# A hybrid S5 / stick-breaking attention block: the scan's preparation in smaller steps, a shorter attention period, and reordered operands in the first up block

## The chip, the cores and the metric

One core of one Trainium2 chip. The metric is the device time of one execution in microseconds (us).

## The reference

One decoder block over 528 positions (512 tokens behind 16 meta tokens), 2048 channels, all in float32:

```python
hn = rmsnorm(h, norm_mix_g[i])
proj = hn @ w_in[i]                       # u 1024 | q k v 1024 each
y_ssm = s5_mixer(u, ...)                  # 64 groups: complex scan of 64 states, GELU, GLU gate
y_attn = stick_breaking_attention(q, k, v).reshape(bsz, L, ATTN_WIDTH)   # 16 heads of 64
mixed = jnp.concatenate([rmsnorm(y_ssm, g_ssm_out[i]), rmsnorm(y_attn, g_attn_out[i])], axis=-1)
h = h + mixed @ w_out[i]
hn = rmsnorm(h, norm_ffn_g[i])
up = causal_depthwise_conv(hn @ w_up[i], conv_w[i], conv_b[i])   # 2 x 5632
gate, val = jnp.split(up, 2, axis=-1)
h = h + (jax.nn.silu(gate) * val) @ w_down[i]
out = rmsnorm(h, norm_final_g)
```

The scan is `h_t = a h_(t-1) + Bbar u_t` with a complex `a` for each state, and `y = Re(C h) + d u`. The attention's weight of a key is `exp(log_sigmoid(z) + sum of log_sigmoid(-z) over the later valid keys)`.

## The kernel before

**Matmuls.** Activations lie with channels on the partitions and positions along the free axis. A float32 product is made of three fp32r matmuls (`mm3`, L317 to L320), which the text calls a triple: high part of the weight by high part of the activation (L318), high by low (L319), low by high (L320). A weight block of 128x1024 is fetched by SyncE's queue (L196), its high part `wh` is a cast on ScalarE (`split_hi`, L240), its low part `wl` a subtraction on VectorE (`split_lo`, by the helper `sub`, L115). `split_high` (L396, ScalarE) and `split_low` (L400, VectorE) do the same for activations that are multiplied by a gain. The helpers at L103 (an activation), L106 (add or subtract), L109 (multiply), L112 (add) and L115 (subtract) record most other operations, so many rows have their lines.

**Order.** Nothing is scheduled by a planner: the order in which the code emits instructions is the order of each engine's queue. The dense work (w_in, w_glu, w_out, up, w_down) is a stream of triples, and beside it runs a lane of other work, written as Python generators. Each triple of which the index in its block is under 7 adds 1.4 times its width to a credit, and when the credit reaches the period, one step of the lane is emitted:

```python
def pulse(ns):
    if hold[0]:
        return
    credit[0] += ns
    while credit[0] >= period[0]:
        credit[0] -= period[0]
        if lanes:
            step()
```

The first lane is the scan (`ssm_lane`, period `PERIOD` = 1600), which begins inside the first blocks of w_in; the second is the attention (`att_lane`, period `PERATT` = 1100); the third makes the operands of the up products (`x_lane`, `PERX` = 1100). Steps rest while the last two blocks of q and the w_glu blocks run. `drain()` (L1298), behind the first half of w_out (the half that multiplies the scan's output), emits all steps that are left of the lanes at once; the second half of w_out multiplies the attention's output.

**Scan.** 64 groups in eight mains `j` of eight groups. `ssm_prep(j)` (L666 to L724) makes the tables of a main on VectorE: rotations `E[c]` (L109 and L106) with a mirrored copy on ScalarE (L103), the decay tile `Dk` (L687), then by `cplx` (L691 ff) four complex products HB[0], HB[1], PB[0], PB[1], each two multiplications (L109) and a sum (L106) into a tile `x` and two ScalarE copies (L704) that set the sum into place; `BB` is set by ScalarE too (L103). `ssm_main(j)` (L726 to L828) transposes PB[0] and PB[1] on TensorE (L735, two times four, each into a bank of PSUM of the pool `z`), copies them out (L737), multiplies, scans on VectorE, multiplies again into Y (L821 to L823), takes the GELU (L103) and stores. A main emits five steps of the next main's preparation: four `next(ahead, None)` between its own steps and the rest by `for _ in ahead: pass` at its end.

**Attention.** Four units of 12 items. `stage_a` makes an item's scores (mask matmul L937, then L953); two steps later `stage_a2` subtracts, scans and subtracts on VectorE (L115 with `at<-z`, L975, L978), which frees the scores' bank; two more steps later `stage_b` transposes (L995, L1005) into a bank of the same pool; then come `stage_c` (L1020, L1044) and `stage_d`. Behind the last item stands the normalisation over 1024 channels: `acc_square` squares on ScalarE and adds on GpSimd (L112), `rms_steps` (L357 to L379) sums over the partitions (L363), takes logarithm and exponent on ScalarE and finishes on VectorE (L367, L374, L109, L379); then for each of eight tiles, one step each, `yatt` is multiplied by the result (L109) and split (L396, L400).

**Up.** The up product runs in 44 blocks f of seven products each (`PROD`: 11, s1, s2, s4, s3, 12, 22), in which sums of weight blocks and of activation blocks are multiplied. In block 0 the sums of activations are made as the block runs: `x_hi` (L1335) casts a high part on ScalarE, `x_lo` (L115) makes a low part on VectorE, sums (L1325, L1330, L115) come ahead of both. In between stands the FFN's normalisation, stepped by `next(norm, None)`.

## Time and profile before

| | |
|---|---|
| median of 3 runs | 2241.73 us (2240.02 to 2243.7) |
| the profiled execution | 2240.49 us |
| its span in the profile | 2238.7 us, 39814 instructions |
| mean granted clock of TensorE | 0.989 of full speed |
| TensorE busy (matmuls / weight loads) | 97% / 92% of the span |
| VectorE busy | 70% |
| ScalarE busy | 47% |
| GpSimd busy | 10% |
| DMA | 335.11 MB, mean 150 GB/s |

The page gives each engine's busy time over the whole span. The list of waits says for what an engine stood still, by the line that waited and the line that released it. A table by stretches gives busy time and granted clock of a part of the span; a clock of 1.00 is full speed. The timeline gives single instructions with start and length, where rows of one line that follow each other are drawn together (x2, x4). A timeline's bracket is the idle time of the engine in front of a row and what ended it.

### The profile page before, as it was taken

What the parts mean: (1) busy time and instruction counts of PE and PEld (TensorE: products, weight loads), DVE (VectorE), ACT (ScalarE), POOL (GpSimd) and SP (SyncE); (2) the same over time, 40 slices, a digit from 0 to 9 for tenths busy, and PEclk for the clock granted to TensorE, in tenths of its full rate; (3) what the DMA queues carried; (4) which work ended last, traced back from release to release, by engine and by line L of the source; (5) the groups of instructions that cost most, each with busy time, mean ns of one, the idle gap of its engine ahead of it and who ended that gap; (6) DMA issues with size and microseconds to landing.
All of it is one profiled execution on the core that took longest, in us unless ns stands there. A gap on an engine that the chain in (4) does not pass through costs nothing.

```text
span 2238.7 us, 39814 instructions
## 1 busy us (share of the span) xinstructions
PE 2170.9 (97%) x16196; PEld 2057.8 (92%) x16196; DVE 1574.1 (70%) x2395; ACT 1042.1 (47%) x1664; POOL 227.6 (10%) x354
## 2 busy tenths in 40 slices
PE   8979999999998999999999999999999999999997
PEld 8979999999897998999999999999999888888887
DVE  7957776775887768887788778877888544444464
ACT  6243443665664445555555555555545222222235
POOL 0000000001222230111011101111110000000004
PEclk9989999999999999999999999999999999999999
DMA  6423223324333256777777677777776533333342
GB/s 214 121 78 100 96 91 111 143 96 143 110 95 109 100 161 169 196 202 188 193 198 203 185 195 199 202 184 196 195 204 189 193 127 116 112 121 116 119 141 76
DMA packets 118807, 335.11 MB, mean 150 GB/s; under 512 B 13024, under 2 KB 25696, under 8 KB 118624
## 3 DMA queue, kind: packets, MB, share of 16 engines
q1 hardware_dynamic: 100288, 269.56, 37.0%
q0 software_dynamic: 17472, 61.89, 13.5%
q8 instruction: 127, 2.08, 0.4%
q10 hardware_dynamic: 864, 1.11, 0.2%
q14 instruction: 56, 0.46, 0.1%
HBM read 300.23 MB, written 32.28 MB: 149 GB/s over the span
## 4 chain that ended last, share of the span: by engine, by line
PE 80%; DVE 4%; ACT 2%; issue 2%; DMA 0%; POOL 0%; DVEq 0%; ACTq 0%; POOLq 0%
PE d L319 19%; PE d L318 19%; PE d L320 19%; PE z L319 4%; PE z L318 4%; PE z L320 4%; PE y L319 2%; PE y L318 2%; PE y L320 2%; PE z L953 1%; DVE wl L115 1%; PE z L1005 1%; PE y L1044 1%; DVE s L115 1%; DVE s L109 1%
## 5 line engine op out<-in xcount | busy, mean ns | idle before, releaser
L318 PE MATMUL d<-s,wh 128*128 128x258 f32 (+4 forms) x3376 | 1038.7, 308 | 14.1 <-ACT s L396 7.2
L319 PE MATMUL d<-s,wh 128*128 128x258 f32 (+4 forms) x3376 | 1033.3, 306 | 8.0 <-DVE s L115 6.4
L320 PE MATMUL d<-s,wl 128*128 128x258 f32 (+4 forms) x3376 | 1028.8, 305 | 0.0
L318 PEld LDWEIGHTS d<-s,wh 128*128 128x128 f32 x3376 | 639.0, 189 | 43.9 <-ACT s L396 7.5
L319 PEld LDWEIGHTS d<-s,wh 128*128 128x128 f32 x3376 | 642.1, 190 | 39.5 <-DVE s L115 7.9
L320 PEld LDWEIGHTS d<-s,wl 128*128 128x128 f32 x3376 | 642.8, 190 | 28.3 <-DVE wl L115 0.2
L240 ACT CAST wh<-wr 128x1024 fp32r<-128x1024 f32 (+2 forms) x209 | 197.5, 945 | 396.7 <-PE d L319 327.6
L115 DVE TENSOR_TENSOR wl<-wr,wh 128x1024 fp32r<-128x1024 f32 (+2 forms) x209 | 233.3, 1116 | 120.7 <-ACT wh L240 109.6
L112 DVE TENSOR_TENSOR s<-s,d 128x512 f32<-128x512 f32 (+2 forms) x176 | 103.4, 589 | 265.0 <-PE d L320 262.4
L319 PE MATMUL z<-s,wh 128*128 128x258 f32 (+1 forms) x752 | 214.9, 286 | 0.0
L318 PE MATMUL z<-s,wh 128*128 128x258 f32 (+1 forms) x752 | 214.1, 285 | 0.0
L320 PE MATMUL z<-s,wl 128*128 128x258 f32 (+1 forms) x752 | 213.2, 284 | 0.0
L318 PE MATMUL y<-s,wh 128*128 128x258 f32 (+1 forms) x640 | 182.9, 286 | 0.0
L319 PE MATMUL y<-s,wh 128*128 128x258 f32 (+1 forms) x640 | 182.3, 285 | 0.0
L320 PE MATMUL y<-s,wl 128*128 128x258 f32 (+1 forms) x640 | 181.1, 283 | 0.0
L115 DVE TENSOR_TENSOR wl<-wu,wh 128x1024 fp32r<-128x1024 f32 x132 | 161.4, 1223 | 5.8 <-ACT wh L240 5.6
L240 ACT CAST wh<-wu 128x1024 fp32r<-128x1024 f32 x132 | 138.9, 1053 | 32.7 <-ACT s L103 32.7
L112 POOL TENSOR_TENSOR s<-s,s 128x514 f32<-128x514 f32 (+1 forms) x73 | 83.3, 1144 | 683.0 <-ACT s L103 545.8
L319 PEld LDWEIGHTS z<-s,wh 128*128 128x128 f32 x752 | 144.5, 192 | 0.0
L320 PEld LDWEIGHTS z<-s,wl 128*128 128x128 f32 x752 | 144.2, 192 | 0.0
L318 PEld LDWEIGHTS z<-s,wh 128*128 128x128 f32 x752 | 142.4, 189 | 0.0
L115 DVE TENSOR_TENSOR wl<-wu_s,wh 128x1024 fp32r<-128x1024 f32 x88 | 107.9, 1226 | 41.4 <-ACT wh L240 41.4
(224 smaller groups left out, 2893.4 us busy)
## 6 DMA issues: line engine op xcount, KB each, us to landing
wu<-w_up SPq DMA_DIRECT2D x132, 512.0 KB, 5.1
wu_s<-w_up SPq DMA_DIRECT2D x88, 512.0 KB, 4.7
wu_s<-w_up POOLq DMA_DIRECT2D x88, 512.0 KB, 7.2
wr<-w_down SPq DMA_DIRECT2D x96, 384.0 KB, 3.0
wr<-w_in SPq DMA_DIRECT2D x63, 512.0 KB, 4.3
wr<-w_out SPq DMA_DIRECT2D x32, 512.0 KB, 3.7
fact<-s POOLq DMA_DIRECT2D x44, 256.0 KB, 2.7
s<-fact SPq DMA_DIRECT2D x44, 256.0 KB, 3.3
```

Source lines behind the costliest of these rows:

```text
L109: e.tensor_tensor(out, a, b, op=ALU.mult)
L112: e.tensor_tensor(out, a, b, op=ALU.add)
L115: e.tensor_tensor(out, a, b, op=ALU.subtract)
L240: S.copy(hi[:, r], raw[:, r])
L318: PE.matmul(ps, whi, xhi, start=start, stop=False, **kw)
L319: PE.matmul(ps, whi, xlo, start=False, stop=False, **kw)
L320: PE.matmul(ps, wlo, xhi, start=False, stop=stop, **kw)
L953: PE.matmul(zs[0][:, x, :], qq[:, i, r], kk[:, :k], start=False, stop=x == nh - 1 and i_ == 2, skip_group_check=True,)
L1005: PE.transpose(b[:, x, :], c[:, P * x : P * x + P], ident[:n, :n])
L1044: PE.matmul(yp[64 * i : 64 * i + 64, p, :], self.vts[p][0][:, t, 64 * i : 64 * i + 64], ws[2 * p + i][:, t, :], start=t == 0 and p == 0, s ...
```

## The change

Four edits. (1) `ssm_prep` is cut into `rotation`, `mirror`, `cplx`, `place` and `place_b`, and has seven steps where it had five: VectorE's sums are emitted one step ahead of the ScalarE copies that read them, with eight `x` tiles in place of four. Three idle steps (`SLACK`) follow the first preparation. In a main, the rest of the next main's preparation is emitted ahead of Y's matmuls, not behind the store. (2) `PERATT` is 950. (3) In the first up block the high parts are cast at j = 0 (before 2), the low parts are made at j = 2 (before 4), and the normalisation's steps begin with the second product. (4) `rms_steps` puts its two half rows into one 528-wide slot, three slots in place of six.

```diff
 NC4 = L // 4
 NEG = -1.0e30
 PERIOD = 1600.0
-PERATT = 1100.0
+PERATT = 950.0
+
+SLACK = 3
 PERX = 1100.0
 HOLD = True
 
...
         def rms_steps(out, acc, parts, width, pool=(psy, "y"), last=()):
 
             n = range(len(parts))
-            v, y, t = [[slot([P, 264])[:, : b - a] for a, b in parts] for _ in range(3)]
+            lo = parts[0][0]
+            v, y, t = [[x[:, a - lo : b - lo] for a, b in parts] for x in [slot([P, 528]) for _ in range(3)]]
             for i, (a, b) in enumerate(parts):
                 ps = bank([P, b - a], *pool)
                 PE.matmul(ps, ones, acc[:, a:b], start=True, stop=not last)
...
             open_phase("ssm")
             yield from ssm_params(SP)
             yield from ssm_prep(0, SP)
+            for _ in range(SLACK):
+                yield
             for j in range(8):
                 while uready[0] <= j:
                     yield
...
             def v4(t):
                 return t.rearrange("p q (a b) -> p q a b", b=12)
 
-            for c in range(2):
+            def rotation(c):
                 ta, tb = slot([P, 4, 72]), slot([P, 4, 72])
                 mul(V, v4(ta), outer(P1[0], 3), outer(P0[c], 2))
                 mul(V, v4(tb), outer(P1[1], 3), outer(P0[1 - c], 2))
                 tt(V, E[c][:, :, MIR:], ta, tb, ALU.subtract if c == 0 else ALU.add)
+
+            def mirror(c):
                 act(E[c][:, :, MIR - 1 :: -1], E[c][:, :, MIR + 1 : 2 * MIR + 1], AF.Copy, scale=1.0 - 2.0 * c)
-                if c == 0:
-                    yield
-            Dk = slot([P, 4, NC4])
-            S.copy(Dk[:, :, 1:], sp["mag4"][:, qs].unsqueeze(2).to_broadcast([P, 4, NC4 - 1]))
-            G.memset(Dk[:, :, 0:1], 0.0)
-            yield
+
             full = [P, 4, 4, 16]
 
             def blk(t):
...
                     t[64 * x : 64 * x + 64].rearrange("p q (s i h) -> p s q i h", s=4, i=2)[:, :, :, x, :] for x in range(2)
                 ]
 
-            def cplx(c, a, b, out):
-
-                t = [small([P, 256], "x", bufs=4).rearrange("p (s q h) -> p s q h", q=4, h=16) for i in range(2)]
+            def cplx(c, a, b):
+
+                t = [small([P, 256], "x", bufs=8).rearrange("p (s q h) -> p s q h", q=4, h=16) for i in range(2)]
                 mul(V, t[0], a[0], b[c])
                 mul(V, t[1], a[1], b[1 - c])
                 tt(V, t[0], t[0], t[1], ALU.subtract if c == 0 else ALU.add)
+                return t[0]
+
+            def place(t, out):
+
                 for hf, r in enumerate(halves):
-                    S.copy(blk(out)[hf], t[0][r])
+                    S.copy(blk(out)[hf], t[r])
+
+            def place_b(c):
+                for x, r in enumerate(halves):
+                    b = sp["bbar"][c][r, qs, :]
+                    act(blk(BB[c])[x], b.unsqueeze(1).to_broadcast([64, 4, 4, 16]), AF.Copy, scale=1.0 - 2.0 * c)
 
             PB, HB, BB = sp["PB"], sp["HB"][j % 2], sp["BB"]
             rep = lambda t: t[:, qs, :].unsqueeze(1).to_broadcast(full)
             kk = [sp["AK"][:, c, 0:4, qs].unsqueeze(3).to_broadcast(full) for c in range(2)]
             rr = [sp["AR"][:, c, :, qs].unsqueeze(3).to_broadcast(full) for c in range(2)]
-            cplx(0, kk, [rep(t) for t in sp["c"]], HB[0])
-            yield
-            cplx(1, kk, [rep(t) for t in sp["c"]], HB[1])
-            for c in range(2):
-                cplx(c, rr, [rep(t) for t in sp["bbar"]], PB[c])
-                for x, r in enumerate(halves):
-                    b = sp["bbar"][c][r, qs, :]
-                    act(blk(BB[c])[x], b.unsqueeze(1).to_broadcast([64, 4, 4, 16]), AF.Copy, scale=1.0 - 2.0 * c)
-                if c == 0:
-                    yield
+            cc, bb = [rep(t) for t in sp["c"]], [rep(t) for t in sp["bbar"]]
+
+            rotation(0)
+            yield
+            rotation(1)
+            mirror(0)
+            Dk = slot([P, 4, NC4])
+            S.copy(Dk[:, :, 1:], sp["mag4"][:, qs].unsqueeze(2).to_broadcast([P, 4, NC4 - 1]))
+            G.memset(Dk[:, :, 0:1], 0.0)
+            yield
+            t0 = cplx(0, kk, cc)
+            mirror(1)
+            yield
+            place(t0, HB[0])
+            t0, t1 = cplx(0, rr, bb), cplx(1, kk, cc)
+            yield
+            place(t0, PB[0])
+            t0 = cplx(1, rr, bb)
+            place(t1, HB[1])
+            place_b(0)
+            yield
+            place(t0, PB[1])
+            place_b(1)
             bt.update(E=E, Dk=Dk, HB=HB)
             yield
 
...
             del loaded[j]
             if uready[0] > j + 1:
                 chunks_in(j + 1)
+            for _ in ahead:
+                pass
             Y = slot([P, 4, NC4])
             for x in range(2):
                 ps = bank([P, 2, NC4], psz, "z")
...
                     PE.matmul(ps[:, q, :], HB[1][:, qq, :], St[1][:, qq, :], start=False, stop=q == 1, skip_group_check=True)
                 act(Y[:, 2 * x : 2 * x + 2, :], ps, AF.Gelu_apprx_tanh)
             nc.sync.dma_start(ydram[j].rearrange("t x q c -> (t x) q c"), Y)
-            for _ in ahead:
-                pass
             yield
 
 
...
                     xh, xl = X[n][j]
                     mm3(ps, w[0][:, j, :], w[1][:, j, :], xh, xl, j == 0 and n in ("11", "s1", "12"), j == 7, skip_group_check=True)
 
+                    if f == 0 and i < 6 and j == 0:
+                        xs = [x_hi(p, PROD[i + 1]) for p in range(EARLY, 8)]
                     if f == 0 and i < 6 and j == 2:
-                        xs = [x_hi(p, PROD[i + 1]) for p in range(EARLY, 8)]
-                    if f == 0 and i < 6 and j == 4:
                         for y in xs:
                             x_lo(*y)
                         if i == 5:
                             xg.clear()
-                        next(norm, None)
+                        if i:
+                            next(norm, None)
                     if j == 3:
                         split_hi(pos[0] + 1)
                         prep(pos[0] + 2)
```

Lines of the changed kernel have other numbers: L704 is L710 there, L240 is L242, L103 is L105, L109 is L111, L112 is L114, L115 is L117, L400 is L403, L374 and L379 are L377 and L382. On TensorE the same rows are emitted; the first transposes L735 stand 20 triples later among the dense ones, the first unit of the attention 21 triples later, and the matmuls of the attention's normalisation 41 triples earlier: 45 triples ahead of the end of the first half of w_out, where there were 4. The attention lane now ends inside that half, and `drain()` finds nothing to emit.

ScalarE, the preparation inside one of the first mains (`s_1505` to `s_1508` are PB and HB tiles, `s_1511` and `s_1512` BB, `wh` a weight's high part, the last two rows the GELU of Y). Before:

```order
L704 COPY s_1507<-x_2913 64x4x4x16 x2
L240 CAST wh_2961<-wr_2743 128x1024
L240 CAST wh_3029<-wr_2857 128x1024
L704 COPY s_1508<-x_3091 64x4x4x16 x2
L704 COPY s_1505<-x_3098 64x4x4x16 x2
L103 ACTIVATE s_1511<-s_1229 64x4x4x16 x2
L240 CAST wh_3113<-wr_2965 128x1024
L704 COPY s_1506<-x_3128 64x4x4x16 x2
L103 ACTIVATE s_1512<-s_1230 64x4x4x16 x2
L103 ACTIVATE s_3151<-z_3152 128x264
L103 ACTIVATE s_3151<-z_3160 128x264
```

The same place in the change (PB and HB are `s_1502` to `s_1505`, BB `s_1508` and `s_1509`):

```order
L242 CAST wh_3010<-wr_2776 128x1024
L242 CAST wh_3078<-wr_2883 128x1024
L242 CAST wh_3146<-wr_3014 128x1024
L710 COPY s_1504<-x_2980 64x4x4x16 x2
L710 COPY s_1502<-x_3161 64x4x4x16 x2
L710 COPY s_1505<-x_3166 64x4x4x16 x2
L105 ACTIVATE s_1508<-s_1226 64x4x4x16 x2
L710 COPY s_1503<-x_3185 64x4x4x16 x2
L105 ACTIVATE s_1509<-s_1227 64x4x4x16 x2
L105 ACTIVATE s_3223<-z_3224 128x264
L105 ACTIVATE s_3223<-z_3232 128x264
L242 CAST wh_3253<-wr_3082 128x1024
```

The three casts stand together ahead of the copies, the copies follow each other without a cast between, and the sums that they read have been emitted a step earlier on VectorE.

VectorE, the end of the attention: last operations of the normalisation (`rstd`), then the eight tiles (`s<-s,rstd` is the multiplication, `vec` the split L400). Before, in one lump behind the first half of w_out:

```order
L379 SCALAR_TENSOR_TENSOR rstd_8893<-s_8898,s_8896 128x258
L379 SCALAR_TENSOR_TENSOR rstd_8893<-s_8899,s_8897 128x256
L109 TENSOR_TENSOR s_8079<-s_8079,rstd_8893 128x514
L109 TENSOR_TENSOR s_8080<-s_8080,rstd_8893 128x514
L400 SCALAR_TENSOR_TENSOR s_8934<-s_8079,vec,s_8933 128x514
L109 TENSOR_TENSOR s_8701<-s_8701,rstd_8893 128x514
L400 SCALAR_TENSOR_TENSOR s_8939<-s_8080,vec,s_8938 128x514
L109 TENSOR_TENSOR s_8703<-s_8703,rstd_8893 128x514
L400 SCALAR_TENSOR_TENSOR s_8944<-s_8701,vec,s_8943 128x514
L109 TENSOR_TENSOR s_8705<-s_8705,rstd_8893 128x514
```

In the change (`s<-d,rstd` is an eviction of w_out's first half, `wl` a weight's low part):

```order
L403 SCALAR_TENSOR_TENSOR s_8797<-s_7970,vec,s_8796 128x514
L111 TENSOR_TENSOR s_8549<-s_8549,rstd_8732 128x514
L403 SCALAR_TENSOR_TENSOR s_8818<-s_7971,vec,s_8817 128x514
L117 TENSOR_TENSOR wl_8845<-wr_8683,wh_8843 128x1024
L111 TENSOR_TENSOR s_8806<-d_8807,rstd_6885 128x258
L111 TENSOR_TENSOR s_8551<-s_8551,rstd_8732 128x514
L403 SCALAR_TENSOR_TENSOR s_8832<-s_8549,vec,s_8831 128x514
L111 TENSOR_TENSOR s_8553<-s_8553,rstd_8732 128x514
L403 SCALAR_TENSOR_TENSOR s_8856<-s_8551,vec,s_8855 128x514
L111 TENSOR_TENSOR s_8555<-s_8555,rstd_8732 128x514
L403 SCALAR_TENSOR_TENSOR s_8867<-s_8553,vec,s_8866 128x514
L111 TENSOR_TENSOR s_8806<-d_8808,rstd_6885 128x256
```

The pairs of multiplication and split now stand between the evictions and the weight subtractions of the first half's last blocks.

VectorE, the first up block, second product: three sums of activations, the two sums of weights `S`, a weight's low part, and the three low parts of the sums (`s<-s,s`). Before:

```order
L115 TENSOR_TENSOR s_10170<-s_9813 128x258
L115 TENSOR_TENSOR s_10174<-s_9950 128x258
L115 TENSOR_TENSOR s_10178<-s_10077 128x258
L112 TENSOR_TENSOR S_10185<-wu_s_9985,wu_11_9921 128x1024
L112 TENSOR_TENSOR S_10189<-S_10185,wu_12_10112 128x1024
L115 TENSOR_TENSOR wl_10191<-S_10185,wh_10187 128x1024
L115 TENSOR_TENSOR s_10172<-s_10170,s_10172 128x258
L115 TENSOR_TENSOR s_10176<-s_10174,s_10176 128x258
L115 TENSOR_TENSOR s_10180<-s_10178,s_10180 128x258
```

In the change:

```order
L117 TENSOR_TENSOR s_10158<-s_9807 128x258
L117 TENSOR_TENSOR s_10162<-s_9944 128x258
L117 TENSOR_TENSOR s_10166<-s_10071 128x258
L117 TENSOR_TENSOR s_10160<-s_10158,s_10160 128x258
L117 TENSOR_TENSOR s_10164<-s_10162,s_10164 128x258
L117 TENSOR_TENSOR s_10168<-s_10166,s_10168 128x258
L114 TENSOR_TENSOR S_10182<-wu_s_9979,wu_11_9915 128x1024
L114 TENSOR_TENSOR S_10186<-S_10182,wu_12_10106 128x1024
L117 TENSOR_TENSOR wl_10188<-S_10182,wh_10184 128x1024
```

The three low parts now stand directly behind the sums, ahead of the sums of weights and the weight's low part.

## Rows read from the trace of the kernel before

**Rows 1.** The page's first part: busy us (share of the span) of each engine.

```profile
PE 2170.9 (97%) x16196; PEld 2057.8 (92%) x16196; DVE 1574.1 (70%) x2395; ACT 1042.1 (47%) x1664; POOL 227.6 (10%) x354
```

**Rows 2.** TensorE's waits over the span: us in total, times, longest.

```profile
PE z L735 <- ACT s L103: 16.1, 6, 6.0
PE d L318 <- ACT s L396: 7.2, 1, 7.2
PE d L319 <- DVE s L115: 6.4, 7, 2.7
PE z L735 <- ACT s L704: 6.4, 2, 5.7
...
PE z L937 <- DVE at L115: 4.0, 2, 3.0
PE y L363 <- POOL s L112: 3.5, 2, 2.4
```

**Rows 3.** Stretches: length; busy of PE, PEld, DVE, ACT, POOL; clock; DMA; GB/s.

```profile
118.50:158.60 40.10, 34.05 (x260) 33.62 (x260) 26.07 (x48) 16.71 (x34) 0.42 (x4) 0.88 0.18 60
158.60:195.80 37.20, 32.37 (x257) 31.94 (x257) 22.84 (x41) 14.95 (x32) 0.21 (x2) 0.96 0.27 87
195.80:295.60 99.80, 94.85 (x775) 93.55 (x775) 74.16 (x132) 44.78 (x94) 0.94 (x9) 0.98 0.30 97
295.60:326.60 31.00, 30.97 (x260) 30.77 (x261) 24.66 (x44) 15.14 (x32) 0.32 (x3) 1.00 0.32 104
...
600.00:716.00 116.00, 115.07 (x1042) 105.88 (x1040) 92.23 (x150) 70.10 (x130) 26.59 (x35) 1.00 0.36 115
716.00:740.00 24.00, 13.97 (x65) 11.78 (x65) 16.43 (x27) 8.34 (x14) 2.65 (x3) 0.72 0.12 43
1000.00:1050.00 50.00, 50.00 (x416) 50.00 (x416) 41.61 (x51) 24.90 (x33) 4.67 (x6) 1.00 0.75 201
828.00:862.50 34.50, 26.76 (x189) 25.82 (x188) 27.04 (x54) 17.95 (x38) 4.48 (x5) 0.90 0.51 130
```

**Rows 4.** Timeline, one main: start, length, engine, line, tiles [idle before <-releaser].

```profile
289.96 1.05 ACT L240 CAST wh<-wr 128x1024 fp32r<-128x1024 f32 x1
...
291.04 1.23 DVE L115 TENSOR_TENSOR wl<-wr,wh 128x1024 fp32r<-128x1024 f32 x1 [2.82 <-ACT wh L240]
...
292.97 0.42 DVE L106 TENSOR_TENSOR x<-x,x 128x256 f32<-128x256 f32 x1
...
293.43 0.82 ACT L704 COPY s<-x 64x256 f32<-64x256 f32 x2 [2.42 <-DVE x L106]
...
295.12 0.67 ACT L103 ACTIVATE s<-z 128x264 f32<-128x264 f32 x2
...
295.57 0.66 PE L735 MATMUL z<-consts,s 128*128 128x128 f32 x4 [1.81 <-ACT s L103]
```

**Rows 5.** Timeline of ScalarE, end of the second main.

```profile
156.83 1.28 ACT L103 ACT_TABLE_LOAD   x1
```

**Rows 6.** Timeline, the attention's end, GpSimd, VectorE and TensorE.

```profile
712.47 4.88 POOL L112 TENSOR_TENSOR s<-s,s 128x514 f32<-128x514 f32 x3 [5.56 <-DVE s L109]
...
712.93 1.92 DVE L115 TENSOR_TENSOR wl<-wr,wh 128x1024 fp32r<-128x1024 f32 x1 [0.54 <-ACT wh L240]
...
725.05 0.75 DVE L400 SCALAR_TENSOR_TENSOR s<-s,vec,s 128x514 fp32r<-128x514 f32 x1 [0.19 <-ACT s L396]
725.72 0.69 DVE L109 TENSOR_TENSOR s<-s,rstd 128x514 f32<-128x514 f32 x1
...
727.22 0.58 PE L318 MATMUL d<-s,wh 128*128 128x258 f32 x1 [7.24 <-ACT s L396]
```

**Rows 7.** Timeline of VectorE, first up block.

```profile
850.20 1.23 DVE L115 TENSOR_TENSOR wl<-wu,wh 128x1024 fp32r<-128x1024 f32 x1 [1.42 <-ACT wh L240]
```

**Rows 8.** Timeline, an attention item: VectorE's subtraction and TensorE's transposes.

```profile
605.34 0.69 DVE L115 TENSOR_TENSOR at<-z,at 128x512 f32<-128x512 f32 x1
...
606.26 0.66 PE L1005 MATMUL z<-consts,at 128*128 128x128 f32 x4
```

## The prediction

> **What bounds the kernel.** I read the page's engine shares first. TensorE is busy 97% of the span and VectorE 70% [rows 1], so a gain can only come from the 3% in which TensorE waits, and from stretches in which its clock is below full. The page cannot say where these lie; the list of TensorE's waits can [rows 2]. The reader is to see there that four causes hold nearly all of it. Before the scan's transposes L735 it waits 16.1 us (6 times) for L103 and 6.4 us (twice) for L704, both ScalarE. It waits once 7.2 us for L396, the first split of the attention's output, 6.4 us (7 times) for the low parts at L115 in the first up block, and 3.5 us for GpSimd's sum at L363. Then I cut the span into stretches, to see what these waits cost with the clock [rows 3].
>
> The main from 295.6 to 326.6 us runs in 31.00 us, with TensorE busy 30.97 of it at full clock. The first main needs 40.10 at a granted clock of 0.88, the second 37.20 at 0.96, the next three together 99.80 at 0.98. Below 1.00 the engine stood for part of the stretch at its lower level (1.2 GHz, not 2.4). Five mains at 31.00 would be 155.0, they take 177.1: **22.1 us** lost. The 6.4 us in front of L735 for L704 belong to the first main, ahead of 118.5 us: **28.5 us** in all for the scan. The end of the attention, 716 to 740 us, is 24.00 us for 65 matmuls at clock 0.72. At full clock a matmul takes 0.12 us (416 in 50.00), so 61 take 7.3 us and the four short ones of L363 about 0.8: some **16 us** lost. From 828.0 to 862.5 us TensorE works 26.76 of 34.50: **7.7 us** lost, at clock 0.90.
>
> **Why the scan waits.** The timeline of one main [rows 4] shows a chain that goes to and fro. ScalarE's cast of a weight (289.96) stands behind the copies of PB[0]; VectorE's subtraction of that weight has waited 2.82 us for it, and only behind it come the products and the sum of PB[1] (292.97), which the copies L704 (293.43) take at once, then BB's copies and the GELU (295.12) that frees the bank of the second four transposes. L735 runs at 295.57, 1.81 us late. In the second main the same queue holds ScalarE's table load too, 1.28 us [rows 5].
>
> **The split preparation and the moved rest.** No operation is added. The diff puts the copies of each result into the step after its sum, with eight x buffers instead of four, so that a tile is not overwritten by the sums that now run ahead. A step is a period of 1600 credits, about 1.6 us of TensorE's work, somewhat more with the eighth triple that is not counted. In [rows 4] the copies start 0.46 us after the sum does, so the step covers it. What is left in front of the bank is ScalarE's own work: two copies (0.82 for both), two of BB (as long), two GELUs (0.67 for both), 2.3 us in all, of which the copies have no late producer any more. The three idle steps and two more steps of preparation start the first main 20 triples later, 20 x 3 x 0.12 = 7.2 us, more than the 6.4 us that it waited. The cover is TensorE's u blocks, which run anyway. If VectorE's parameter work is behind by more than 7.2 us there, the rest of the wait stays. Five steps of a main are still executed from inside the main, now the last ones before Y's matmuls: what is queued behind them on TensorE is Y, and they put no matmul ahead of it, so it waits for nothing new. Of the 28.5 us I leave 1.28 for the table load and one cast of 1.05 that may still stand before a GELU: gain **26 us**. Bounds: 28.5 if nothing stays, 6.4 if only the first main is cured.
>
> **Period 950.** The attention lane starts 21 triples later, but its normalisation comes 41 triples earlier, 41 x 0.36 = 14.8 us: 45 triples, 16.2 us of matmuls, remain in the first half of w_out instead of 4, and nothing is left for the lump at the end. VectorE must do in them four pairs of normalisation operations on half rows (some 0.67 a pair, as from 725.05 to 725.72 for one whole row, 2.7), eight multiplications and eight splits, 1.27 us for two from start to start (0.69 and 0.75 long, [rows 6]), 10.2, and what the first half itself puts between them: two subtractions of 1.23 and four evictions of about 0.42, 4.1. That is 17.0 against 16.2 us, with L363's wait for GpSimd (3.5 us in two places, of which the longest, 2.4, is the other) in front. I expect L396's 7.2 us and the low clock behind it to go, and 5 us to stay: gain **11 us**, bounds 8 and 15. What is late next is the last L403 (L400 before).
>
> That sum hangs on VectorE. Its subtraction at 712.93 took 1.92 us beside GpSimd's three additions (4.88 us), not 1.23 as alone [rows 4, 6]: 0.7 more for one, and there will be some three such meetings, 2 us, which is in the 5. The Trainium skill, "SBUF — State Buffer", section "SBUF: two separate sides", speaks against this edit: a VectorE operation with two SBUF inputs and a GpSimd operation that reads SBUF exclude each other for a whole instruction. By that, three additions of 1.6 would hold VectorE up 4.9 us instead of 2, and the tail would gain 8; the row, where 0.7 of a possible 1.6 was lost, agrees in kind and not in full.
>
> The price is paid in the attention items. Two steps are 300 credits shorter, 0.3 us. Transposes L1005 need the bank that the subtraction two steps earlier frees; where that is tight (the subtraction of 605.34 takes 0.69 and ends 0.23 us before L1005 at 606.26, [rows 8]) the wait begins; most others that I looked at had more. If one in six of 48 items loses its full 0.3, that is 2.4: **2.5 us** lost. Bounds: 0, and 48 x 0.3 = 14.4. The lane does its work in 545 triples instead of 607; if it makes a third of VectorE's 92.23 us in 116 (80%, [rows 3]), the share becomes 83%, which still holds.
>
> **First up block.** The high parts are cast at j = 0 instead of 2 and the low parts made at 2 instead of 4; the normalisation starts one product later, 2.9 us, and its result is needed only about 10 us behind its end. VectorE idled 1.42 us before a subtraction because ScalarE's cast came after the x casts ([rows 7], three such, and two of 0.5: 5.3 in all). With both earlier by two triples (0.72 us), about 1.1 of that stays. VectorE's 27.04 us against TensorE's 26.76 in this stretch [rows 3] leave little else to win: gain **4 us** (bounds 0, and 7.7).
>
> The three shared slots of the normalisation change addresses, not work. They cost nothing while the next user of those slots is later than the last reader, which is the rstd step; without that cover it would be one VectorE step of 0.7 us, twice.
>
> **Sum.** 26 + 11 + 4 - 2.5 = 38.5. The profiled run took 2240.49 us, 1.8 more than its span and 1.2 below the median of the three runs (2241.73): 2240.5 - 38.5 = **2202**.
>
> **Rivals.**
> A, as above: 2194 to 2210, about 8 us either way, since the terms (the tail 3 or 4, the up block 4, scan and items 2.5 each) seldom err together.
> B, everything comes back: the scan 28.5, the tail 15, the up block 7.7, the items lose nothing: 51, about 2189. For it: the mains without waits show that the scan can run at 31.00. Against: VectorE at 80 to 85%.
> C, the banks bind at every item: 14.4 instead of 2.5, 2214. For it: the gap of 0.23 us at 606. Against: most items had more, and TensorE waits only 0.93 us in 600 to 716.
> D, the scan's waits only move: VectorE's sums still stand behind a subtraction whose cast is behind more copies (six rows of the order now follow each other without a cast between). If half of the 22.1 stays, 2213; if all but the first main's 6.4 stays, about 2222, and with the tail's lower bound and C's price 2236. For it: the 2.82 us wait is a matter of order on ScalarE, and casts still share its queue. Against: the copies are a step late by design.
> E, slower. The clock falls in the attention stretch, now at 1.00. More frequent steps bring short waits back at each item; suppose each costs one fall to 1.2 GHz, as the one in the third of the scan's stretches, where a clock of 0.98 over 99.80 us [rows 3] is 2.0 us of lost work. It decides from about 22 of 48 items on: 22 x 2.0 = 44, the whole gain of 38.5 and the 4.5 that tell a loss from no change (below); 2246. Against: a wait of 3.0 us at L937 [rows 2] brought no fall. The Trainium skill, "TensorE: Matmul & The Clock Gate", section "HAM oscillation — how this bites in real kernels", tells of a loop whose waits recur and lose the clock at each turn; here only the scan's longer waits show it.
> F, the change does not do what it says, since the order on the engines came out alike or the terms cancel: 2240. The order of instructions shows the move, so this is slight.
>
> **How the numbers follow.** A 0.60, B 0.13, C 0.13, D 0.09, E 0.03, F 0.02. The range 2186 to 2222 holds A, B, C and the better half of D, and leaves out the rest, under 0.2. No change means within 0.2%, about 4.5 us, which is what this kernel's measurement can tell. A to D are all faster, 0.95, of which I take 0.01 away for D's worst end: faster 0.94, same 0.02, slower 0.04.
>
> **What would show it.** Right: the L735 waits under 4 us in all, the first two mains near 32 us at clock 0.98 or more; the wait for L396 gone and at most 4 us at the last L403; 716 to 740's low clock gone; under 3 us of L115 waits in the up block; L1005 on the list with 2 or 3 us. Wrong: L735 still above 10 us (D), L1005 above 8 us (C), clock under 0.97 between 600 and 716 (E), or 5 us and more for the last split, which would make the tail's term too large.

## The result and the profile after

The changed kernel takes **2210.60 us** (median of 4 runs, 2209.55 to 2212.19), the kernel before 2241.36 on the same chips: a ratio of 0.9862, with a 95% interval of 0.9845 to 0.9879, 30.8 us less. The forecast of 2202 had the sign and the range right (2186 to 2222) and was 8.6 us too low. The profiled execution took 2212.19 us against 2240.49, 28.3 less.

The page's first part, as [rows 1]: the busy times are those of before, only the span is shorter.

```profile
PE 2167.5 (98%) x16196; PEld 2055.5 (93%) x16196; DVE 1576.3 (71%) x2395; ACT 1040.3 (47%) x1664; POOL 227.6 (10%) x354
```

TensorE's waits over the span of the changed kernel, as [rows 2]:

```profile
PE z L961 <- DVE at L117: 5.7, 5, 3.3
PE d L320 <- ACT wh L242: 5.7, 1, 5.7
PE z L1019 <- DVE at L117: 4.3, 3, 2.2
PE y L366 <- DVE s L114: 2.9, 1, 2.9
PE d L321 <- DVE s L403: 1.7, 3, 0.8
```

The scan's transposes (L759 now) are gone from the list, 22.5 us before, and so is the first split L399 (7.2). What is new stands at the attention: L961, the mask matmul of an item's scores, and L1019, the transposes of a unit's last item. The 5.7 us for a weight's cast are the start of the kernel, as before (5.4).

Stretches of the changed kernel, as [rows 3] (length; busy of PE, PEld, DVE, ACT, POOL; clock; DMA; GB/s): six scan mains, the attention up to its normalisation, its end, the first up block.

```profile
121.40:152.10 30.70, 30.67 (x257) 30.48 (x256) 26.53 (x48) 15.82 (x32) 0.24 (x3) 1.00 0.34 114
152.10:182.90 30.80, 30.77 (x260) 30.57 (x259) 24.57 (x44) 14.86 (x32) 0.30 (x3) 1.00 0.32 104
182.90:276.00 93.10, 93.01 (x780) 92.42 (x779) 72.14 (x130) 45.41 (x94) 0.73 (x9) 1.00 0.32 105
276.00:306.90 30.90, 30.87 (x260) 30.67 (x259) 24.43 (x44) 14.10 (x31) 0.24 (x3) 1.00 0.30 99
...
341.10:681.00 339.90, 327.44 (x2814) 305.72 (x2813) 249.62 (x409) 206.79 (x387) 53.48 (x104) 0.98 0.34 112
681.00:729.40 48.40, 45.19 (x351) 44.07 (x350) 32.24 (x54) 19.92 (x33) 13.19 (x11) 0.96 0.31 108
804.90:840.90 36.00, 31.30 (x237) 29.28 (x236) 33.44 (x62) 21.95 (x45) 4.51 (x5) 1.00 0.59 153
```

The same three stretches of the kernel before, which [rows 3] did not hold, the attention, its end and the first up block:

```profile
361.60:710.90 349.30, 342.47 (x2997) 321.88 (x2996) 255.14 (x420) 210.41 (x391) 56.86 (x106) 1.00 0.36 118
710.90:756.40 45.50, 35.47 (x244) 33.28 (x243) 28.92 (x47) 17.77 (x32) 10.60 (x9) 0.85 0.21 75
829.20:865.20 36.00, 28.26 (x201) 27.32 (x200) 29.62 (x58) 19.00 (x39) 4.48 (x5) 0.91 0.50 126
```

Every main now runs in some 31 us at full clock, the first too. The attention went the other way: 6.83 us idle at clock 1.00 before, 12.46 at 0.98 now.

To compare kernels by stretch, I call **loss** TensorE's idle time by this view plus half of what it worked at the lower clock. An example is the attention's end before: of 45.50 us it is idle for 10.03, and of the 13.65 us at 1.2 GHz (725.06 to 738.71) it works 9.88, so the loss is 10.03 + 4.94 = 15.0. Before and after: scan 29.5 and 0.2; attention 6.8 and 18.6; its end 15.0 and 4.9; first up block 10.9 and 4.7; and the input's first normalisation, 1.4 and 4.6, where this execution had a wait of 2.9 us and a fall of the clock that most other runs of this code lack. Together that is 30.5 less, beside the 28.3 measured.

The measure is good to a few us. With all losses taken off the span, the fourteen profiles of this document leave between 2152 and 2159 us for the same matmuls, where one number should stand.

A timeline of one main after, as [rows 4]: PB[1]'s sum (L108), its copies (L710), BB's, the GELU, the next cast, and the transposes.

```profile
303.45 0.42 DVE L108 TENSOR_TENSOR x<-x,x 128x256 f32<-128x256 f32 x1
...
304.12 0.82 ACT L710 COPY s<-x 64x256 f32<-64x256 f32 x2
...
304.95 0.84 ACT L105 ACTIVATE s<-s 64x256 f32<-64x256 f32 x2
305.82 0.67 ACT L105 ACTIVATE s<-z 128x264 f32<-128x264 f32 x2
306.48 0.90 PEld L759 LDWEIGHTS z<-consts,s 128*128 128x128 f32 x8
306.52 1.05 ACT L242 CAST wh<-wr 128x1024 fp32r<-128x1024 f32 x1
306.59 1.03 PE L759 MATMUL z<-consts,s 128*128 128x128 f32 x8
```

The copies wait for nothing (no bracket, 2.42 us before), and the cast stands behind the GELU.

Two counts ahead of the prediction are off. The preparation has six steps in place of five, not seven; and a main has five `next(ahead, None)`, so the loop over `ahead` had nothing left before and emits the sixth step now. The 20 triples were read from the order and stand: three idle steps and one more of preparation, not two.

### The profile page after: what moved, and what is told of

The parts are those of the page before. It is cut to its first block, busy times and chain, and to the rows that moved or that the text cites. A ratio compares the mean times of both kernels' runs of the same rounds, so it can differ in the third digit from the quotient of the medians.

```text
span 2210.4 us, 39830 instructions
## 1 busy us (share of the span) xinstructions
PE 2167.5 (98%) x16196; PEld 2055.5 (93%) x16196; DVE 1576.3 (71%) x2395; ACT 1040.3 (47%) x1664; POOL 227.6 (10%) x354
## 4 chain that ended last, share of the span: by engine, by line
PE 63%; DVE 2%; issue 1%; ACT 1%; POOL 0%; DVEq 0%; ACTq 0%; POOLq 0%
PE d L321 15%; PE d L320 15%; PE d L322 15%; PE z L321 4%; PE z L320 4%; PE z L322 4%; PE y L321 2%; PE y L320 2%; PE y L322 2%; DVE s L117 0%; DVE wl L117 0%; DVE s L114 0%; ACT wh L242 0%; DVE s L111 0%; ACT s L1359 0%
## 5 line engine op out<-in xcount | busy, mean ns | idle before, releaser
L242 ACT CAST wh<-wr 128x1024 fp32r<-128x1024 f32 (+2 forms) x209 | 197.6, 946 | 428.1 <-PE d L321 337.4
L117 DVE TENSOR_TENSOR wl<-wr,wh 128x1024 fp32r<-128x1024 f32 (+2 forms) x209 | 231.5, 1108 | 88.1 <-ACT wh L242 87.8
L114 DVE TENSOR_TENSOR s<-s,d 128x512 f32<-128x512 f32 (+2 forms) x176 | 103.6, 590 | 263.3 <-PE d L322 253.0
L320 PE MATMUL y<-s,wh 128*128 128x258 f32 (+1 forms) x656 | 186.5, 284 | 0.0
L321 PE MATMUL y<-s,wh 128*128 128x258 f32 (+1 forms) x656 | 186.1, 284 | 0.0
L117 DVE TENSOR_TENSOR wl<-wu,wh 128x1024 fp32r<-128x1024 f32 x132 | 161.4, 1223 | 3.3 <-ACT wh L242 2.7
L114 POOL TENSOR_TENSOR s<-s,s 128x514 f32<-128x514 f32 (+1 forms) x73 | 83.4, 1143 | 697.5 <-ACT s L105 582.7
L242 ACT CAST wh<-wu 128x1024 fp32r<-128x1024 f32 x132 | 138.8, 1052 | 32.5 <-ACT s L105 32.4
L117 DVE TENSOR_TENSOR wl<-wu_s,wh 128x1024 fp32r<-128x1024 f32 x88 | 107.9, 1226 | 41.3 <-ACT wh L242 41.3
```

Source lines behind the costliest of these rows:

```text
L114: e.tensor_tensor(out, a, b, op=ALU.add)
L117: e.tensor_tensor(out, a, b, op=ALU.subtract)
L242: S.copy(hi[:, r], raw[:, r])
L320: PE.matmul(ps, whi, xhi, start=start, stop=False, **kw)
L321: PE.matmul(ps, whi, xlo, start=False, stop=False, **kw)
```

## The experiments

The losses by stretch in each profile, in us, with where the attention's lane begins (in triples of the dense work; its first matmuls stand 19 to 24 triples later, at 821 before and 838 after) and its period. The medians come from several sessions, in which the kernel before had 2241.4 to 2243.4 us, so the ratios compare better than the times:

| kernel | median | start, period | scan | attention | end | up block |
|---|---|---|---|---|---|---|
| before | 2241.4 | 797, 1100 | 29.5 | 6.8 | 15.0 | 10.9 |
| after | 2210.6 | 818, 950 | 0.2 | 18.6 | 4.9 | 4.7 |
| after, period 1100 | 2225.2 | 818, 1100 | 1.4 | 23.8 | 18.5 | 5.4 |
| before, period 950 | 2251.4 | 797, 950 | 29.0 | 27.1 | 4.8 | 10.9 |
| after, old up block | 2216.9 | 818, 950 | 0.8 | 19.8 | 4.3 | 10.3 |
| after, no idle steps | 2219.7 | 803, 950 | 5.7 | 27.5 | 7.1 | 4.7 |
| after, last item later | 2213.5 | 818, 950 | 1.1 | 19.5 | 7.2 | 4.7 |
| the same, first too, 920 | 2211.2 | 818, 920 | 0.9 | 15.8 | 7.6 | 4.7 |
| after, rest behind store | 2210.1 | 818, 950 | 0.7 | 18.7 | 3.2 | 5.4 |
| after, copies with sums | 2212.2 | 818, 950 | 7.0 | 18.5 | 3.2 | 5.4 |
| before, four idle steps | 2236.1 | 818, 1100 | 10.1 | 23.5 | 18.0 | 10.5 |
| after, copies with sums, no idle | 2227.4 | 803, 950 | 11.3 | 26.2 | 4.2 | 5.5 |
| after, period 900 | 2217.0 | 818, 900 | 0.9 | 26.5 | 2.9 | 5.5 |
| after, start as before, 1100 / 850 | 2207.7 | 797, 1100 | 0.4 | 15.2 | 8.5 | 4.7 |

The expectations count small gaps between TensorE's rows as well, some 9 us more in the attention's stretch than this table.

**The period alone, both ways.**

```diff
-PERATT = 950.0
+PERATT = 1100.0
```

> The changed kernel with the attention period back at 1100; the rest of the change stays. In the trace of the changed kernel TensorE loses, by idle time and half of its busy time at the lower clock, 39 us between 360 and 700 us, against 26 before, and 6 between 700 and 745, against 17. Theory T1 (the shorter period itself costs the attention items their slack): the loss between 360 and 700 goes back to about 26, and the lump behind the first half of w_out returns (a loss of 16 to 18 around its end), so that the two nearly cancel: 2209 to 2213 us. Rival T2 (the lane's later start, 21 triples, moves its unit boundaries onto other dense work, and the period is not to blame): the attention keeps some 39, the lump comes on top, 2221 to 2225. In both the scan's transposes wait for nothing.

2225.21 us, ratio to before 0.9919 (0.9906 to 0.9932): 14.6 us above the change's median. The lump is back (L399 6.7 us), and the attention does not recover: 23.8, more than at 950. T1 falls here; the time is the one of T2.

```diff
-PERATT = 1100.0
+PERATT = 950.0
```

> The kernel before with the attention period at 950 alone. T1: the attention's stretch loses 13 us more, the end of the attention 11 less or a little better (its normalisation stands 62 triples earlier than in the kernel before), so 2239 to 2243 us, about no change. T2: the attention's stretch loses as before, and the end of the attention gains 11 to 15: 2226 to 2230. The scan's waits stay at 22 us in both.

2251.39 us, 1.0042 (1.0029 to 1.0056): slower than before, outside both. The end gains 10.2, as it does in the change, but the attention loses 20.3 more. So neither the period nor the start alone carries the loss: at the early start 1100 is far the better, at the late start 950 is.

**The first up block.**

```diff
-                    if f == 0 and i < 6 and j == 0:
+                    if f == 0 and i < 6 and j == 2:
...
-                    if f == 0 and i < 6 and j == 2:
+                    if f == 0 and i < 6 and j == 4:
...
-                        if i:
-                            next(norm, None)
+                        next(norm, None)
```

> The changed kernel with the first up block's operands in the order of before. If the reordering brought what its stretch shows (a loss of 9 instead of 14 us between the attention and the second up block), 2214 to 2216 us and L117 waits of 5 to 6 us in that block again; if that stretch's difference comes from elsewhere, 2210 to 2212.

2216.93 us, 0.9886 (0.9872 to 0.99): 6.3 us above the change's median, 5.4 by the ratios, and the block's loss is 10.3 in place of 4.7. The reordering is worth some 5 to 6. Its waits for the low parts (4.7 us) and for GpSimd's sum at L366 (2.4 us) are back.

**The scan.** Three edits, one at a time and then two together.

```diff
-SLACK = 3
+SLACK = 0
```

> The changed kernel without the three idle steps. If the idle steps cover the first main's wait: the first transposes L759 wait 3 to 5 us again, perhaps with a fall of the clock, and the whole attention lane stands 15 triples earlier; 2211 to 2217 us. If the two added steps of the preparation and the earlier sums are enough without them: no wait at L759, 2207 to 2211.

2219.67 us, 0.9894 (0.9878 to 0.991). That is above both ranges. The scan loses 5.7, with 2.9 us of waits at the first main's L759, so the idle steps do cover the first main. The attention, which now starts at 803, loses 8.9 more, which is more than either range had allowed for.

```diff
-            for _ in ahead:
-                pass
             Y = slot([P, 4, NC4])
...
             nc.sync.dma_start(ydram[j].rearrange("t x q c -> (t x) q c"), Y)
+            for _ in ahead:
+                pass
             yield
```

> The changed kernel with the last preparation steps of a main again behind the store, where they stood before. The forecast put the cure of the scan on the copies' later step, not on this move. If so: L759 waits under 2 us in all, 2209 to 2214 us. If the move matters (PB[1]'s copies now stand behind Y's GELUs, and the next main's transposes come soon after): 1 to 2 us at each of seven mains, 2218 to 2225 us.

2210.14 us, 0.9853 (0.9839 to 0.9868), and 0.7 in the scan: the move does nothing.

```diff
             t0 = cplx(0, kk, cc)
             mirror(1)
+            place(t0, HB[0])
             yield
-            place(t0, HB[0])
-            t0, t1 = cplx(0, rr, bb), cplx(1, kk, cc)
             yield
+            t0, t1 = cplx(0, rr, bb), cplx(1, kk, cc)
             place(t0, PB[0])
-            t0 = cplx(1, rr, bb)
             place(t1, HB[1])
             place_b(0)
             yield
+            t0 = cplx(1, rr, bb)
             place(t0, PB[1])
```

> The changed kernel with the ScalarE copies of HB and PB in the step of their sums again; the seven steps, the three idle ones and the rest before Y stay. If the copies' later step is the cure: L759 waits 10 us or more in all, with falls of the clock in the first mains, 2222 to 2235 us. If the idle steps and the finer steps are: 2209 to 2214 us.

The edit takes the sums to the step of their copies, so the fourth of the six steps is left empty. 2212.21 us, 0.9866 (0.9851 to 0.988), in the second range: by time it is not told apart from the change. The scan's loss is 7.0. The waits at L759 make up 2.5 of it, three of under 1 us. The largest wait is of another kind, for a load of u:

```profile
125.62 3.61 PE L779 MATMUL z<-s,s 128*128 128x132 f32 x16 [2.75 <-DMA s<-udram]
```

With the fall of the clock beside it, it makes 4.4. The kernels of this table that start as late and make the sums a step earlier wait 0 to 1.2 us there. So the forecast's cure is worth at most 7 us of 29, not nearly all.

```diff
             yield from ssm_prep(0, SP)
+            for _ in range(4):
+                yield
```

> The kernel before with four idle steps behind the first preparation, so that its scan and its attention start where the changed kernel's do (period 1100, old preparation). With the copies one step late no longer shown as the sole cure, two readings of the scan's 22 to 28 us: S1 (the mains themselves go to and fro, in each one): the first main's 6.4 us go, the later waits stay, a loss of 20 us or more in the scan's stretch. S2 (a backlog of VectorE from the scan's parameters, which the idle steps let it work off before the first main): a loss under 12 us. The attention's stretch should lose 33 as with the late start and period 1100, 18 more than before, and its end 4 more, in both. So S1: 2250 to 2258 us, S2: 2238 to 2246 us.

2236.13 us, 0.9974 (0.9964 to 0.9984), below both. With the old preparation four idle steps alone take the scan's loss from 29.5 to 10.1, S2's size. The waits at the scan's transposes go from 22.1 us between 100 and 346 us (15.7 for L103, 6.4 for L704) to 3.7, and 4.4 of the 10.1 are again a wait for a load of u (2.67 us at L757, 126.03) with a fall of the clock. Its first five mains by stretch:

```profile
119.00:157.10 38.10, 32.62 (x256) 32.04 (x255) 28.27 (x50) 17.51 (x35) 0.24 (x3) 0.95 0.28 92
157.10:189.50 32.40, 32.37 (x258) 32.17 (x259) 24.73 (x44) 15.06 (x32) 0.28 (x3) 0.95 0.31 97
189.50:282.60 93.10, 93.01 (x780) 92.42 (x779) 72.21 (x129) 45.40 (x95) 0.88 (x9) 1.00 0.33 104
```

The end of the second main of the kernel before (Y's first product, the cast between PB[0] and PB[1], the transposes):

```profile
147.07 0.39 PE L821 MATMUL z<-s,s 128*128 128x132 f32 x2
...
151.68 1.05 ACT L240 CAST wh<-wr 128x1024 fp32r<-128x1024 f32 x1
...
158.57 0.69 PE L735 MATMUL z<-consts,s 128*128 128x128 f32 x2 [6.02 <-ACT s L103]
```

The same place with four idle steps:

```profile
149.55 0.39 PE L823 MATMUL z<-s,s 128*128 128x132 f32 x2
...
149.87 1.04 ACT L240 CAST wh<-wr 128x1024 fp32r<-128x1024 f32 x1
...
157.10 1.11 PE L737 MATMUL z<-consts,s 128*128 128x128 f32 x4 [2.80 <-ACT s L103]
```

The chain to and fro is there in both, 6.9 and 7.2 us from the cast to the transposes. What differs is how far the lane's VectorE and ScalarE work runs ahead of TensorE: the cast starts 4.6 us behind Y's first matmul in the one, 0.3 in the other. With enough of a lead the chain costs nothing: the next three mains run in 31.0 each. That the lead is what counts is read from these rows and argued from them; TensorE's stop at the load of u, 4.4 us, adds to VectorE's lead here.

```diff
-SLACK = 3
+SLACK = 0
```

on top of the copies in the sums' step:

> The changed kernel with the copies in the step of their sums and without the three idle steps: both cures of the scan gone, the six smaller steps, the period of 950, the up block's order stay. Alone the first brought the scan's loss from 1.6 to 9 us, the second to 7.6. If they stand in for each other (S2: either is enough to hold the backlog off): the scan loses 20 us or more again, 2230 to 2240 us. If they only add: about 15 us, 2224 to 2229 us. If neither matters beside the finer steps: 2217 to 2222 us.

2227.39 us, 0.9937 (0.9922 to 0.9952), in the range for cures that add. The scan loses 11.3, where 15 had been expected. By the table the idle steps are worth 4.2 to 5.5 and the later copies 5.6 to 6.8. By time the later copies are worth 1.6 us with the idle steps (not clear of noise) and 7.7 without them, so "they add" is the table's reading.

The 18 us left, between 29.5 and 11.3, came with what this kernel still has. Smaller steps are not among it, as the expectation had it: its six steps are the old five with an empty one put in, the mirrored copies a step behind their rotations, and the last step just ahead of Y. So there is left one step more ahead of the first main, the places of these steps in a main, and eight x tiles for four. The tiles can be left out, since VectorE's list of waits before has none for L704 between 100 and 330 us. The others were not tried apart; that four idle steps with the old five take away 19 speaks for the later start.

**Where the attention loses.** In the changed kernel the three longest waits are these:

```profile
549.86 0.56 PE L1019 MATMUL z<-consts,at 64*128 64x64 f32 x5 [2.21 <-DVE at L117]
...
568.57 0.39 PE L961 MATMUL z<-mask,identb 128*128 128x256 bf16 x1 [3.32 <-DVE at L117]
...
617.54 0.52 PE L1019 MATMUL z<-consts,at 64*128 64x64 f32 x5 [1.85 <-DVE at L117]
```

All stand at a unit's boundary: the last item's transposes, which meet the next unit's preparation, and the scores of a new unit's third item. VectorE ahead of the second one, from its timeline:

```profile
561.49 1.23 DVE L117 TENSOR_TENSOR wl<-wr,wh 128x1024 fp32r<-128x1024 f32 x1 [4.45 <-ACT wh L242]
...
563.43 1.40 DVE L111 TENSOR_TENSOR s<-s,s 128x258 f32<-128x258 f32 x1
564.86 1.39 DVE L382 SCALAR_TENSOR_TENSOR rstd<-s,s 128x258 f32<-128x258 f32 x1
566.17 0.74 DVE L999 SCALAR_TENSOR_TENSOR at<-z,at 116x256 f32<-116x256 f32 x2
...
568.12 0.72 DVE L117 TENSOR_TENSOR at<-z,at 116x256 f32<-116x256 f32 x2
```

It stood 4.45 us for a weight's cast, then had the normalisation of the scan's output (L370 to L382, belonging to w_out's second block), and only then the first item's chain, whose end frees the bank that L961 wants.

```diff
+                    e = 2 if it is None else 0
-                    for lag, f in ((A2, un.stage_a2), (B, un.stage_b), (C, un.stage_c)) + (((C + 2, un.stage_d),) if it is None else ()):
+                    for lag, f in ((A2, un.stage_a2), (B + e, un.stage_b), (C + e, un.stage_c)) + (((C + 2 + e, un.stage_d),) if it is None else ()):
```

> The changed kernel with one thing moved: the last item of each attention unit (the 16-position item, whose transposes L1019 waited 2.2 and 1.9 us) has its transposes, products and squares two steps later. Theory T3 (what the attention loses are the unit boundaries: this item's chain on VectorE falls into the same steps as the next unit's preparation, so its transposes come too early; which period or start catches them worst is chance): the L1019 waits go, with the clock falls at 550 and 618 us, 4 us of waits and 3 to 4 us of clock: 2202 to 2206 us. Rival T4 (the attention is short of VectorE time throughout, and a wait taken away here returns at the next item): 2209 to 2213 us.

2213.52 us, 0.9867 (0.985 to 0.9883): no gain, the loss in the attention is 19.5. The L1019 waits went, and 2.25 us at L1029, 3.25 at L920 and 2.33 at L961 came. T4 for this edit: the wait moves on.

```diff
-                    yield from tick(2)
+                    yield from tick(3 if n == 0 else 2)
...
-PERATT = 950.0
+PERATT = 920.0
```

> As the one before, with a step more behind each unit's first item (whose banks the third item's mask matmul L961 waited 3.3 us for) and a period of 920, which puts the normalisation at the same place. T3: the L961 waits go as well and the attention's stretch loses under 20 us in place of 28: 2198 to 2204. T4: the loss stays above 26, or grows with the shorter period: 2208 to 2216.

2211.18 us, 0.9859 (0.9844 to 0.9874): no difference from the change. The time is T4's. The attention's loss is 15.8, with one fall of the clock in place of three (some 25 as the expectation counts, between T3's 20 and T4's 26), but its end loses 7.6 in place of 4.9.

```diff
-PERATT = 950.0
+PERATT = 900.0
```

> The changed kernel with the attention period at 900. If a shorter period takes slack from each item, the attention's stretch loses 32 us or more in place of 28, and its end gains nothing: 2213 to 2222 us. If the loss follows from which steps of the lane meet which dense work (the same start lost 28 at 950 and 34 at 1100), it may go either way by 5 to 10 us: 2202 to 2220 us, with the long waits at other items than 549.9, 568.6 and 617.5.

2216.97 us, 0.989 (0.9875 to 0.9905), which lies in both ranges. The loss is 26.5 in the attention, with a wait of 6.05 us at the next unit's transposes L917 (558.9 us), and the end hardly better (2.9). At the late start 950 lies between two worse periods.

```diff
-PERATT = 950.0
+PERATT = 1100.0
+PERLAST = 850.0
...
-            yield
+            if j < 7:
+                yield
...
+                if u == 3:
+                    period[0] = PERLAST
```

(the last main's step is left out at four places in this way).

> The changed kernel with the attention put back to where the kernel before had it: four idle steps are left out in the scan's last main (which prepares nothing), so that the attention's first matmuls stand as many triples into the dense work as before; the period is 1100 for the first three units and 850 from the last unit on. Its normalisation stands 26 triples earlier than before, 15 later than in the change. Theory T5 (what the attention loses is set by where its unit boundaries fall among the dense blocks; the same start and period give the same loss): the stretch up to its normalisation loses 16 to 22 us, as before (15.5) and a little for the faster last unit, and its end 8 to 12: 2200 to 2207 us, better than both. T4 (with the scan's time taken out, VectorE is behind whatever the start): 26 us or more there, 2209 to 2218 us. If leaving out idle steps of the last main brings scan waits back, they show at the last L759.

2207.73 us, 0.9844 (0.9831 to 0.9858): 2.9 below the change, with intervals that overlap, so better than before and not told apart from the change. The time lies between T5's range and T4's and decides nothing; the attention loses 15.2, of which 1.67 us are a wait at Y's matmul L852 (359.47), behind the steps left out of the last main. What decides is where it waits. From its timeline:

```profile
432.46 0.51 PE L1023 MATMUL z<-consts,at 64*128 64x64 f32 x5 [1.03 <-DVE at L118]
...
543.68 1.66 PE L945 MATMUL z<-s,qt 128*64 128x264 f32 x12 [0.70 <-DVE at L118]
...
571.62 0.40 PE L965 MATMUL z<-mask,identb 128*128 128x256 bf16 x1 [3.04 <-DVE at L118]
```

and those of the kernel before at the same places:

```profile
457.18 0.52 PE L995 MATMUL z<-consts,at 64*128 64x64 f32 x5 [1.04 <-DVE at L115]
...
569.15 1.66 PE L917 MATMUL z<-s,qt 128*64 128x264 f32 x12 [0.74 <-DVE at L115]
...
597.10 0.28 PE L937 MATMUL z<-mask,identb 128*128 128x256 bf16 x1 [3.05 <-DVE at L115]
```

The same three waits to 0.04 us, in a kernel that is 25 us earlier and has another scan: T5, for the waits. (The clock differs, see the last section.) The other pairs say the same: 1100 from 818 on lost 23.8 and 23.5 with two different preparations (the longest wait 4.15 us at the same transposes in both), 950 from 803 on 27.5 and 26.2. From 818 on at 950, four kernels that leave the attention's code alone (the change, the old up block, the rest behind the store, the copies with the sums) lost 18.5 to 19.8. Where the last experiment loses more than the kernel before, 15.2 against 6.8, it is the wait at Y, a fall of the clock (2.9), and from the last unit on, at 850, more waits (1.60 and 1.35 us are the longest).

## Why the forecast was right, and where it was off

**Scan: 26 forecast, 29.3 measured.** The chain to and fro was read rightly and its cure wrongly shared out. That the sum still came out is in part luck: both cures were in the same edit. "Two copies ... of which the copies have no late producer any more" is worth 7 us at most. The step that failed is pricing the later start at the first main's 6.4 alone: four idle steps take away 19. VectorE's lead over TensorE is carried from main to main: with four idle steps the second main takes 32.40 us in place of 37.20 and the next three 93.1 in place of 99.8. The 1.28 for the table load and 1.05 for a cast, which I had left in, do not show either: the table load is hidden (no L759 wait at all), the cast stands behind the GELU. Rival D did not come.

**End of the attention: 11 forecast, 10.1 measured; first up block: 4 forecast, 6.2 measured,** and 5.6 by undoing it. The up block's sum priced idle time alone: 3.0 of the 6.2 are idle time, and 3.2 are the clock, 0.91 before and 1.00 after. GpSimd's sum at L363, for which TensorE had waited 2.4 us there, was not priced either; that wait is gone, and 4.6 us of new ones have come (2.9 for weights' low parts, 1.7 for copies at L1434). The end's working held: L399 no longer waits, the splits L403 make TensorE wait 1.7 us, and one fall of the clock is left. It hung on GpSimd as feared, at two places, of which this is one and the second is like it (1.79 beside an addition of 1.68 at 704.39):

```profile
694.04 1.68 POOL L114 TENSOR_TENSOR s<-s,s 128x514 f32<-128x514 f32 x1 [6.95 <-DVE s L111]
...
694.48 1.80 DVE L403 SCALAR_TENSOR_TENSOR s<-s,vec,s 128x514 fp32r<-128x514 f32 x1
...
704.83 1.79 DVE L403 SCALAR_TENSOR_TENSOR s<-s,vec,s 128x514 fp32r<-128x514 f32 x1
...
706.67 0.39 PE L321 MATMUL d<-s,wh 128*128 128x258 f32 x1 [0.79 <-DVE s L403]
```

A split of 0.75 us ends 0.56 behind the end of GpSimd's addition, so it cost 1.05 each, 2.1 in all, near the 2 taken. The Trainium skill, "SBUF — State Buffer", section "SBUF: two separate sides", has the two engines exclude each other for a whole instruction. By that the split would end 0.75 us behind the addition; here the trace agrees to 0.2 us, where the row ahead of the prediction had shown it in part.

**Attention: 2.5 forecast, 11.8 measured.** This is the step that made the time too low. "Transposes L1005 need the bank that the subtraction two steps earlier frees" is not where it went: L1029, as they are now, has no wait of 0.5 us or more in the changed kernel. The loss stands at the unit boundaries, which the forecast did not look at, as about half waits (12.46 idle against 6.83) and half clock (13.7 us at 1.2 GHz, 6.2 lost, against none). Its size is near rival C's bound of 14.4, its place is not C's; and E's mechanism is real in part: three falls stand beside the waits of 2.21, 3.32 and 1.85 us, far from the 22 that would have decided. Nor is it the shorter period as such. With the late start, which the scan's edit brings, going back to 1100 loses more.

The terms' errors add up: 3.3 and 2.2 better, 9.3 and 0.9 worse, and 3.3 worse at the first normalisation of this execution, together 8.0 worse. The profiled execution came out 10.2 above the forecast, the median 8.6; the rest is within what this measure can tell. So errors of 5.5 one way and 13.5 the other cancelled in part, and the forecast was nearer than its attention term deserved.

**What stays open:** which of one later step and the steps' places in a main took the scan's first 18 us; what the shared slots of edit (4) do, since no run undoes them alone; why the same wait costs the clock in one kernel and not in another; and which start and period are best together, since only three starts were run, and few periods from each.

## What to carry to other kernels

Where a lane of side work is emitted by a counter beside dense work, its start and its period have to be chosen together, and again after every edit ahead of it: here the same period of 950 lost 18.6 us from one start and 26 to 28 from two others, while kernels with the same start and period, and the same attention code, lost the same to 1.3 us. Before a to-and-fro chain is taken apart, try a few idle steps ahead of it: how far the producer's engine runs ahead may decide more than the chain's length, as four idle steps did here (19 us of 29).

## What the runs showed of the chip that was not expected

The same wait can cost the clock or not. The 3.05 us at 597.10 in the kernel before left TensorE at 2.4 GHz (granted clock 1.00 from 361.6 to 710.9). The 3.04 us at the same place in the last experiment, at 571.62, went with a stretch of 6.8 us at 1.2 GHz. And in the changed kernel 1.85 us (617.54) were followed by 3.4 us at 1.2 GHz. The kernel before had shown as much in its first up block, where the forecast (rival E) saw such falls behind the scan's longer waits only: waits of 2.36 us (833.22) and 2.71 us (851.81) each stand beside 3.4 us at 1.2 GHz. A forecast that prices such a wait needs both cases.
